# A two-layer trunk on one core: bias lines made by copies, small loads later, and three pieces of the schedule moved

## The chip, the cores and the metric

The kernel runs on one core of a Trainium2 chip. The metric is the device time of the whole execution in microseconds, as the median of several runs. One execution was also taken by the hardware profiler; its span runs from the first to the last instruction.

## The reference, cut to what matters

256 tokens of width 1024 pass two layers. Layer 0 is differential attention with eight pairs of heads, layer 1 is block attention, which at 256 tokens (one block) is plain causal attention with 16 heads on keys and values made from the stream. Each is followed by a squared-ReLU MLP of width 4096. Every softmax gets a bias from one table of 32 buckets by 16 heads, looked up by the distance of query and key; from a distance of 113 on, all fall into the last bucket.

```python
n = jnp.maximum(rel, 0)                       # rel = qpos - kpos
large = max_exact + (jnp.log(nf / max_exact) / math.log(128 / max_exact) * 16).astype(jnp.int32)
bucket = jnp.where(n < max_exact, n, jnp.minimum(large, 31))
...
# layer 0, per pair of heads m = 0, 1
s = einsum(q, k) + rel_bias[bucket]; s = where(rel >= 0, s, -inf); p = softmax(s)
a = p[:, :, 0] - lam * p[:, :, 1]
o = einsum(a, v)
o = o * rsqrt(mean(o * o) + eps) * subln_g * (1 - lam_init)
h = layer_norm(alpha * h + o @ w_out)
h = layer_norm(alpha * h + square(relu(h @ w_up)) @ w_down)
# layer 1: the same with plain softmax on shared keys and values
```

## The kernel before

All weights stream through on-chip memory as 96 units of 128 x 2048 fp32, each in two pieces of 128 x 1024. A product in fp32 is made of three matmuls in the fast fp32r format: a weight is split into `whi` (a rounded copy, by ACT, ScalarE) and `wlo` (what is left, by DVE, VectorE, as a subtraction), and an activation into `act_hi` and `act_lo` likewise. `three` (L134) issues the three matmuls, `fetch` (L82) loads a raw piece on SyncE's queue (SP) into one of five buffers, and `piece` (L103) splits one: it makes whi of this piece and the next on ACT, then wlo on DVE, then fetches the fifth piece on. `bg` calls it as often as the schedule says there, up to seven units ahead of use.

Nothing reorders the program: each engine runs its instructions as the code was written, so where a call stands in the code is where its parts stand on all engines. Transfers signal eight completion semaphores in turn (DMAHW0 to DMAHW7 in the listings), whether SP's or ACT's queue issued them.

The first two units are treated apart, by `v_first`: in eight chunks, k = 0 to 7, of 256 columns of x (transposed, `xT`) and 512 of the weight. For each, ACT makes act_hi and whi, DVE act_lo and wlo, and TensorE runs six matmuls of 512 columns. Ahead of that stands the head: DVE clears 512 columns (`zero`) and fills a table, TensorE runs four warm-up matmuls on the zeros (L177), the 33 x 384 one-hot matrix and the bias table are loaded on ACT's queue, and a matmul of the two (L183) gives for each of the 16 heads one line of 384 biases, by distance; the last 128 are the mask. DVE copies it out (L184), chunk 0 writes it to memory (`scr`, L363), and `load_bias` later reads from it, row by row one element further on, the 128 x 256 bias tile of a pair. The lambda vectors are loaded by GpSimd's queue at the start.

Attention in layer 0 goes by pairs of heads: `project` makes q and k, `halves_hi` and `halves_lo` split them, `scores` multiplies, `softmax_a` adds the bias and takes the maxima (DVE, L461 and L464) and the exponentials (ACT, L470), `softmax_b` puts the two maps together into `t` (DVE, L482), `turn` transposes t on TensorE (L503), `turned` copies that out as `aT`, and `values` multiplies with V (L527 to L529). Pairs 0 to 3 gather in O[0]: `rms` squares O (eight ACT operations, L563) and takes the reciprocal root on GpSimd (L253 and on), `scale` multiplies it in on DVE (L569), and `o_turn` transposes the scaled O on TensorE (L276) and splits it into act_hi (ACT) and act_lo (DVE, L73) for the output projection, `mix`.

In layer 1, `softmax_b` is a reciprocal and four scalings on DVE (L491, L494). In the MLP, `square` is a relu and a square on ACT (L737, L739), and `up_turn` transposes the result (L760).

Of the kernel before, what the change touches and what calls it, by code (L numbers as in the profile page):

```python
# [20 lines left out]
F32 = mybir.dt.float32  # L21
# [7 lines left out]
P = 128  # L29
D = 1024  # L30
# [3 lines left out]
NBUCKET = 32  # L34
# [18 lines left out]
def trunk(ctx: ExitStack, tc: tile.TileContext, x, xT, units, lam_a, subln, rel_bias,  # L53
          ln_g, ln_b, ident_in, onehot, out):
# [100 lines left out]
    early = wpool.tile([P, 2, D], F32, name="lnp").rearrange("p a b -> p (a b)")  # L155
    zero = early[:, 1024:1536]
    nc.vector.memset(zero, 0.0)
    oh = early[:, :RELS]
    table = const.tile([NBUCKET + 1, NH], F32, name="table")
    nc.vector.memset(table, 1.0)  # L160
    nc.scalar.dma_start(table[:NBUCKET], rel_bias)
    nc.scalar.dma_start(oh[:NBUCKET + 1], onehot)
    xres = const.tile([P, 2, D], F32, name="xres")
    xTr = xres.rearrange("p a b -> p (a b)")
    for k in range(NK):
        if k % 2 == 0:
            raws[k // 2] = wpool.tile([P, PIECE], F32, name="raw", bufs=RAWS)
        nc.sync.dma_start(xTr[:, k * S:(k + 1) * S], xT[:, k * S:(k + 1) * S])
        nc.sync.dma_start(raws[k // 2][:, (k % 2) * 512:(k % 2 + 1) * 512],
                          units[k // 4][:, (k % 4) * 512:(k % 4 + 1) * 512])  # L170
    fetch(4)
    ident = const.tile([P, P], F32, name="ident")
# [8 lines left out]
    pb = bank("c")  # L181
# [17 lines left out]

    def make_lambda():  # L200
        nc.gpsimd.dma_start(la, bass.AP(tensor=lam_a.tensor, offset=lam_a.offset,
                                        ap=[[0, P], [64, 4], [1, 64]]))
        nc.gpsimd.dma_start(gsub, subln.rearrange("o p -> p o"))
# [118 lines left out]
    def attention(layer, u0):  # L322
# [4 lines left out]
        with tc.tile_pool(name=f"attn{layer}", bufs=2) as pool, \  # L327
# [19 lines left out]
            def v_first(u):  # L347
# [7 lines left out]
                for k in range(4):  # L355
# [6 lines left out]
                    if kk == 0:  # L362
                        nc.scalar.dma_start(scr, line)  # L363
# [3 lines left out]
                    if kk < 2:  # L367
                        nc.tensor.matmul(warm[:, :P], zero[:, :P], zero[:, :P], start=True, stop=True)
# [8 lines left out]
            if layer == 0:  # L377
# [3 lines left out]
                nc.sync.dma_start(ident, ident_in)  # L381
                free.update(used)
# [242 lines left out]
            if diff:  # L625
# [48 lines left out]
            else:  # L674
# [16 lines left out]
                bg(2, True)  # L691
                softmax_b(7)
                values(6)
# [30 lines left out]
    def mlp(layer, u0, then):  # L724
# [3 lines left out]
        with tc.tile_pool(name=f"mlp{layer}", bufs=2) as pool:  # L728
# [87 lines left out]
            for g in range(2):  # L816
                up_rows(0, 1, g)
                bg(2)
# [151 lines left out]
```

## Time and profile before

| | us |
|---|---|
| median of 3 runs | 612.29 |
| lowest, highest | 611.0, 615.39 |
| the profiled execution | 612.53 |
| its span | 610.7 |
| TensorE busy in the span | 598.1 (98%), 3774 instructions |
| DVE, ACT, GpSimd busy | 379.4, 319.1, 9.8 |
| mean granted clock of TensorE | 0.995 of full |

TensorE is busy nearly all the time; the other engines have room on average, though not in each stretch. What lies outside the span is 1.8 us.

### The profile page before, as it was taken

How to read it: one execution, taken by the hardware profiler on the slowest of the kernel's cores; microseconds unless marked ns; L12 is line 12 of the kernel's file. 1: busy time of each engine (PE TensorE's matmuls, PEld its weight loads, DVE VectorE, ACT ScalarE, POOL GpSimd, SP SyncE). 2: the span in 40 equal slices, each digit the busy share in tenths (PEclk: the TensorE clock that was granted, in tenths of full speed). 3: DMA queues.
4: the chain of work that ended last, by engine and by line, in shares of the span. 5: the costliest groups of instructions: out<-in, count | busy, mean ns of one | idle time of the engine just before them, and what ended most of it. 6: DMA issues, size and time to landing. Idle time of an engine off the chain costs nothing.

```text
span 610.7 us, 9663 instructions
## 1 busy us (share of the span) xinstructions
PE 598.1 (98%) x3774; PEld 525.5 (86%) x3774; DVE 379.4 (62%) x694; ACT 319.1 (52%) x540; POOL 9.8 (2%) x29
## 2 busy tenths in 40 slices
PE   9999999999999999999999999999999999999994
PEld 6899987889898899898889999878798899899884
DVE  5597778976734734643777677687586544544236
ACT  5676687447654654552336555542686554564200
POOL 0000020000000000000000000000000000000000
PEclk9999999999999999999999999999999999999997
DMA  7996664547656657556149745151688556553001
GB/s 227 334 335 215 210 215 162 179 143 267 210 208 212 197 182 241 200 181 207 59 157 313 279 155 160 52 173 34 210 307 287 189 176 211 174 171 104 1 0 69
DMA packets 36408, 113.09 MB, mean 185 GB/s; under 512 B 3899, under 2 KB 9708, under 8 KB 36364
## 3 DMA queue, kind: packets, MB, share of 16 engines
q1 hardware_dynamic: 35008, 108.08, 53.0%
q0 software_dynamic: 1232, 4.33, 2.1%
q8 instruction: 29, 0.48, 0.3%
q10 hardware_dynamic: 124, 0.08, 0.1%
q14 instruction: 15, 0.12, 0.1%
HBM read 111.40 MB, written 1.07 MB: 184 GB/s over the span
## 4 chain that ended last, share of the span: by engine, by line
PE 79%; issue 9%; DMA 4%; DVE 3%; ACT 2%; POOL 1%; SPq 0%; DVEq 0%; POOLq 0%; ACTq 0%
PE ps_a L139 12%; PE ps_a L140 12%; PE ps_a L138 12%; PE ps_b L142 10%; PE ps_b L144 10%; PE ps_b L143 10%; PE ps_b L140 3%; PE ps_b L138 3%; PE ps_b L139 3%; DMA raw<-in_units 3%; DVE wlo L112 1%; PE ps_c L276 1%; PE ps_a L450 1%; PE ps_c L503 1%; DMA bias<-scr 1%
## 5 line engine op out<-in xcount | busy, mean ns | idle before, releaser
L112 DVE TENSOR_TENSOR wlo<-raw,whi 128x1024 fp32r<-128x1024 f32 x188 | 222.8, 1221 | 62.0 <-ACT whi L100 61.6
L100 ACT ACTIVATE whi<-raw 128x1024 fp32r<-128x1024 f32 x188 | 190.1, 1053 | 81.0 <-PE ps_a L140 50.5
L142 PE MATMUL ps_b<-act_hi,whi 128*128 128x256 f32 x640 | 182.4, 285 | 0.0
L144 PE MATMUL ps_b<-act_hi,wlo 128*128 128x256 f32 x640 | 180.2, 282 | 0.8 <-DVE wlo L112 0.8
L143 PE MATMUL ps_b<-act_lo,whi 128*128 128x256 f32 x640 | 179.9, 281 | 0.0
L142 PEld LDWEIGHTS ps_b<-act_hi,whi 128*128 128x128 f32 x640 | 120.5, 188 | 1.8 <-issue 0.7
L144 PEld LDWEIGHTS ps_b<-act_hi,wlo 128*128 128x128 f32 x640 | 120.5, 188 | 1.0 <-DVE wlo L112 1.0
L143 PEld LDWEIGHTS ps_b<-act_lo,whi 128*128 128x128 f32 x640 | 120.5, 188 | 0.5
L138 PE MATMUL ps_a<-whi,h_hi 128*128 128x512 f32 x248 | 98.5, 397 | 0.0
L140 PE MATMUL ps_a<-whi,h_lo 128*128 128x512 f32 x248 | 98.3, 396 | 0.0
L139 PE MATMUL ps_a<-wlo,h_hi 128*128 128x512 f32 x248 | 98.3, 396 | 0.0
L71 DVE TENSOR_TENSOR h_lo<-sqr,h_hi 128x512 fp32r<-128x512 f32 x24 | 16.6, 692 | 80.0 <-ACT h_hi L69 80.0
L140 PEld LDWEIGHTS ps_a<-whi,h_lo 128*128 128x128 f32 x248 | 46.7, 188 | 11.3
L139 PEld LDWEIGHTS ps_a<-wlo,h_hi 128*128 128x128 f32 x248 | 46.8, 189 | 10.8
L138 PEld LDWEIGHTS ps_a<-whi,h_hi 128*128 128x128 f32 x248 | 46.7, 188 | 10.8
L737 ACT ACTIVATE relu<-ps_b 128x512 f32<-128x512 f32 x32 | 19.1, 596 | 67.9 <-PE ps_b L144 57.7
L470 ACT ACTIVATE t<-t,mx 128x256 f32<-128x256 f32 x64 | 28.4, 445 | 30.9 <-DVE mx L467 30.9
L138 PE MATMUL ps_b<-whi,act_hi 128*128 128x512 f32 x96 | 39.2, 409 | 0.4 <-ACT act_hi L69 0.4
L140 PE MATMUL ps_b<-whi,act_lo 128*128 128x512 f32 x96 | 38.0, 396 | 0.5 <-DVE act_lo L73 0.5
L139 PE MATMUL ps_b<-wlo,act_hi 128*128 128x512 f32 x96 | 37.9, 395 | 0.0
L138 PE MATMUL ps_a<-whi,act_hi 128*128 128x512 f32 x80 | 32.4, 405 | 0.0
L140 PE MATMUL ps_a<-whi,act_lo 128*128 128x512 f32 x80 | 31.6, 395 | 0.0
(137 smaller groups left out, 591.7 us busy)
## 6 DMA issues: line engine op xcount, KB each, us to landing
raw<-in_units SPq DMA_DIRECT2D x188, 512.0 KB, 4.9
bias<-scr SPq DMA_DIRECT2D x16, 256.0 KB, 5.0
raw<-in_units SPq DMA_DIRECT2D x8, 256.0 KB, 5.5
lnp<-in_ln_g POOLq DMA_DIRECT2D x4, 512.0 KB, 3.9
lnp<-in_ln_b POOLq DMA_DIRECT2D x4, 512.0 KB, 5.1
xres<-in_xT SPq DMA_DIRECT2D x8, 128.0 KB, 4.4
xres<-in_x SPq DMA_DIRECT2D x1, 1024.0 KB, 6.8
out<-xres SPq DMA_DIRECT2D x2, 256.0 KB, 2.0
```

The source lines that it names most:

```text
L71: nc.vector.tensor_tensor(lo, src, hi.bitcast(F32), op=ALU.subtract)
L100: nc.scalar.activation(split[v][0][:, c], raws[state["head"]], AF.Copy)
L112: nc.vector.tensor_tensor(split[v][1][:, c], raws.pop(state["piece"]), split[v][0][:, c].bitcast(F32), op=ALU.subtract)
L138: nc.tensor.matmul(ps, a[0], w[0], start=start, stop=False)
L139: nc.tensor.matmul(ps, a[0], w[1], start=False, stop=False)
L140: nc.tensor.matmul(ps, a[1], w[0], start=False, stop=stop)
L142: nc.tensor.matmul(ps, w[0], a[0], start=start, stop=False)
L143: nc.tensor.matmul(ps, w[0], a[1], start=False, stop=False)
L144: nc.tensor.matmul(ps, w[1], a[0], start=False, stop=stop)
L276: nc.tensor.transpose(pt[:, j * P:(j + 1) * P], src[:, j * P:(j + 1) * P], ident)
L470: nc.scalar.activation(t[:, m, s], t[:, m, s], AF.Exp, bias=mx[:, m, j:j + 1], accum_out=sm[:, m, j:j + 1])
L737: nc.scalar.activation(r, ps, AF.Relu)
```

## The change

Four things change. **The head:** the first weight chunk is issued on ACT's queue; the one-hot matrix, its matmul, the copy and the table's filling go; the bias table, transposed to 16 x 32, is loaded behind that chunk on ACT's queue; and GpSimd builds the lines, with a memset for the mask, sixteen copies of one bucket's column over the run of distances that it covers, and one copy of sixteen buckets in reverse. Only 256 columns are cleared. The write of the lines moves from chunk 0 to chunk 6, the two warm matmuls inside chunks 0 and 1 go, and the lambda loads move to SP's queue, behind the identity matrix.

**The end of attention 0:** `rms` of O[0] moves ahead of a `bg(1)` and `softmax_b(6)`, `o_turn(0, ...)` moves ahead of the values of pairs 4 to 6, two pieces instead of three stand behind it, and the values of pairs 4 to 7 stand together ahead of `mix`. **Attention 1:** of two pieces ahead of `softmax_b(7)`, one moves behind it. **The MLP:** two pieces behind the last rows of the first chunk move behind `square` and `up_turn`.

```diff
-    oh = early[:, :RELS]
-    table = const.tile([NBUCKET + 1, NH], F32, name="table")
-    nc.vector.memset(table, 1.0)
-    nc.scalar.dma_start(table[:NBUCKET], rel_bias)
-    nc.scalar.dma_start(oh[:NBUCKET + 1], onehot)
...
-        nc.sync.dma_start(raws[k // 2][:, (k % 2) * 512:(k % 2 + 1) * 512],
-                          units[k // 4][:, (k % 4) * 512:(k % 4 + 1) * 512])
+        (nc.sync if k else nc.scalar).dma_start(raws[k // 2][:, (k % 2) * 512:(k % 2 + 1) * 512],
+                                                units[k // 4][:, (k % 4) * 512:(k % 4 + 1) * 512])
     fetch(4)
...
+    zero = early[:, 1024:1280]
+    nc.vector.memset(zero, 0.0)
+    table = early[:NH, :NBUCKET]
...
-    nc.tensor.matmul(pb[:NH, :RELS], table, oh[:NBUCKET + 1], start=True, stop=True)
-    nc.vector.tensor_copy(line, pb[:NH, :RELS])
+    def make_lines():
+        nc.scalar.dma_start(table, rel_bias)
+        nc.gpsimd.memset(line[:, 256:], MASKED)
+        b, half = _buckets(), NBUCKET // 2
+        runs = [j for j in range(256 - half) if j == 0 or b[j] != b[j - 1]] + [256 - half]
+        for c, d in zip(runs, runs[1:]):
+            nc.gpsimd.tensor_copy(line[:, c:d], table[:, b[c]:b[c] + 1].to_broadcast([NH, d - c]))
+        nc.gpsimd.tensor_copy(line[:, 256 - half:256], table[:, :half][:, ::-1])
...
+    def load_lambda():
+        nc.sync.dma_start(la, ...)
+        nc.sync.dma_start(gsub, subln.rearrange("o p -> p o"))
...
-                    if kk == 0:
+                    if kk == 6:
                         nc.scalar.dma_start(scr, line)
...
-                    if kk < 2:
-                        nc.tensor.matmul(warm[:, :P], zero[:, :P], zero[:, :P], start=True, stop=True)
...
                 nc.sync.dma_start(ident, ident_in)
+                load_lambda()
...
                 turned(5)
+                scale = rms(0, [O[0][:, h] for h in range(2)], nc.gpsimd)
                 bg(1)
                 softmax_b(6)
-                scale = rms(0, [O[0][:, h] for h in range(2)], nc.gpsimd)
                 bg(1)
...
                 turn(7)
-                for p in range(4, 7):
-                    values(p)
                 turned(7)
-                bg(3, True)
                 o_turn(0, 0)
                 o_turn(0, 1)
-                values(7)
+                bg(2, True)
+                for p in range(4, 8):
+                    values(p)
                 mix(0, 0, G0)
...
-                bg(2, True)
+                bg(1, True)
                 softmax_b(7)
+                bg(1, True)
...
-            for g in range(2):
-                up_rows(0, 1, g)
-                bg(2)
+            up_rows(0, 1, 0)
+            bg(2)
+            up_rows(0, 1, 1)
             SQ[0, 1] = square(SQ[0, 1])
             up_turn(1, 0)
+            bg(2)
```

ACT's first instructions before; `raw` is a weight chunk, `lnp` the buffer that holds one-hot matrix, lines and zeros, and what a row waits for stands in brackets:

```order
L162 DMA lnp<-in_onehot 33x384
L161 DMA table<-in_rel_bias 32x16 [waits DVE_49]
L69 ACT_TABLE_LOAD
L69 ACTIVATE act_hi<-xres 128x256 [waits DMAHW1_49]
L69 ACTIVATE whi<-raw 128x512 [waits DMAHW2_49]
L363 DMA scr<-lnp 16x384 [waits DVE_49]
L69 ACTIVATE act_hi<-xres 128x256 [waits DMAHW4_49]
L69 ACTIVATE whi<-raw 128x512 [waits DMAHW5_49]
```

The first five of them now, and, where the dots are, chunks 1 to 5 left out, the part around the write:

```order
L161 DMA raw<-in_units 128x512
L180 DMA lnp<-in_rel_bias 16x32
L69 ACT_TABLE_LOAD
L69 ACTIVATE act_hi<-xres 128x256 [waits DMAHW1_49]
L69 ACTIVATE whi<-raw 128x512 [waits DMAHW0_49]
...
L69 ACTIVATE whi<-raw 128x512 [waits DMAHW6_49]
L369 DMA scr<-lnp 16x384 [waits Pool_49]
L69 ACTIVATE act_hi<-xres 128x256 [waits DMAHW7_49]
L69 ACTIVATE whi<-raw 128x512 [waits DMAHW0_49]
L100 ACTIVATE whi<-raw 128x1024 [waits DMAHW1_49]
```

The write moved from behind chunk 0 to behind chunk 6 and waits for GpSimd instead of DVE; behind it stand chunk 7's two splits and the first whole piece.

ACT at the end of attention 0 before, from the copy of pair 5's aT to the exponentials of pair 7 (L470):

```order
L512 ACTIVATE aT<-ps_c 128x384 [waits PE_49]
L100 ACTIVATE whi<-raw 128x1024 [waits DMAHW2_49]
L563 ACTIVATE sq,ss<-o 128x128 [waits Activation_49]
L563 ACTIVATE sq,ss<-o 128x128
L563 ACTIVATE sq,ss<-o 128x128 [waits Activation_49] x6
L100 ACTIVATE whi<-raw 128x1024 [waits DMAHW5_49]
L512 ACTIVATE aT<-ps_c 128x384 [waits PE_49]
L470 ACTIVATE t,sm<-t,mx 128x256 [waits DVE_49]
```

The same stretch now:

```order
L517 ACTIVATE aT<-ps_c 128x384 [waits PE_49]
L568 ACTIVATE sq,ss<-o 128x128 [waits Activation_49]
L568 ACTIVATE sq,ss<-o 128x128
L568 ACTIVATE sq,ss<-o 128x128 [waits Activation_49] x6
L100 ACTIVATE whi<-raw 128x1024 [waits DMAHW3_49]
L100 ACTIVATE whi<-raw 128x1024 [waits DMAHW6_49]
L517 ACTIVATE aT<-ps_c 128x384 [waits PE_49]
L475 ACTIVATE t,sm<-t,mx 128x256 [waits DVE_49]
```

The eight squares moved ahead of the first of two whi. On DVE the wlo of that piece stands directly ahead of pair 7's maxima (L466 and L469), in both kernels; now:

```order
L112 TENSOR_TENSOR wlo<-raw,whi 128x1024 [waits DMAHW3_49,Activation_49]
L466 ISA t,mx<-ps_a,bias 128x256 [waits DMAHW5_49,PE_49]
L466 ISA mx 128x1
L469 ISA t,mx<-ps_a,bias 128x128
L469 ISA mx 128x1
```

Nothing moved in these five rows; the whi that the first of them waits for did.

TensorE a little later before, from the transposes of pair 7's t (L503) over the values of pairs 4 to 6 and O's eight transposes to the values of pair 7 and `mix`:

```order
L503 MATMUL ps_c<-ident,t 128x128 x3
L527 MATMUL ps_a<-V,aT 128x128
L528 MATMUL ps_a<-V,aT 128x128
L529 MATMUL ps_a<-V,aT 128x128
...
L276 MATMUL ps_c<-ident,o 128x128 x8
L527 MATMUL ps_a<-V,aT 128x128
L528 MATMUL ps_a<-V,aT 128x128
L529 MATMUL ps_a<-V,aT 128x128
L138 MATMUL ps_b<-whi,act_hi 128x512
```

Now:

```order
L508 MATMUL ps_c<-ident,t 128x128 x3
L282 MATMUL ps_c<-ident,o 128x128 x8
L532 MATMUL ps_a<-V,aT 128x128
L533 MATMUL ps_a<-V,aT 128x128
L534 MATMUL ps_a<-V,aT 128x128
...
L138 MATMUL ps_b<-whi,act_hi 128x512
```

O's transposes moved directly behind those of t, and all four groups of values stand between them and `mix`.

## Rows read from the trace of the kernel before

**Rows 1.** Waits of TensorE: operand, line, awaited engine: total us, times, longest.

```profile
PE ps_c L177 <- DVE table L160: 1.4, 1, 1.4
...
PE ps_c L760 <- ACT sqr L739: 0.3, 1, 0.3
```

**Rows 2.** Timeline of the head: start us, us, engine, line, operation, count, [idle before <-releaser].

```profile
1.16 0.43 SPq L169 DMA_DIRECT2D raw<-in_units  x1
...
1.44 3.78 PE L177 MATMUL ps_c<-lnp 128*128 128x256 f32 x8 [1.44 <-DVE table L160]
...
3.43 0.42 ACT L69 ACTIVATE act_hi<-xres 128x256 fp32r<-128x256 f32 x1 [0.34 <-DMA xres<-in_xT]
...
5.75 0.63 ACT L69 ACTIVATE whi<-raw 128x512 fp32r<-128x512 f32 x1 [1.91 <-DMA raw<-in_units]
...
6.54 1.22 PE L366 MATMUL ps_a<-whi,act_hi 128*128 128x512 f32 x2
...
8.85 1.05 PE L372 MATMUL ps_a<-wlo,act_hi 128*128 128x512 f32 x2
...
9.70 1.03 PE L366 MATMUL ps_a<-whi,act_hi 128*128 128x512 f32 x2
...
11.26 0.63 PE L372 MATMUL ps_a<-wlo,act_hi 128*128 128x512 f32 x2
...
11.72 0.63 PE L366 MATMUL ps_a<-whi,act_hi 128*128 128x512 f32 x2
...
19.06 1.06 ACT L100 ACTIVATE whi<-raw 128x1024 fp32r<-128x1024 f32 x1 [0.86 <-DMA raw<-in_units]
...
21.44 0.39 PE L144 MATMUL ps_b<-act_hi,wlo 128*128 128x256 f32 x1 [0.76 <-DVE wlo L112]
```

**Rows 3.** Transfers of the first 40 us: total; issue: count, KB each, us to landing.

```profile
DMA packets 5401, 11.36 MB, mean 284 GB/s; under 512 B 647, under 2 KB 2598, under 8 KB 5399
...
table<-in_rel_bias ACTq DMA_DIRECT2D x1, 2.0 KB, 3.2
```

**Rows 4.** Timeline of the end of attention 0, columns as in rows 2.

```profile
83.86 0.30 ACT L563 ACTIVATE sq<-o 128x128 f32<-128x128 f32 x1
...
85.33 0.42 DVE L461 CUSTOM_DVE_ANT_0 t<-ps_a,bias 128x256 f32<-128x256 f32 x1
...
86.20 1.05 ACT L100 ACTIVATE whi<-raw 128x1024 fp32r<-128x1024 f32 x1
...
87.52 0.51 ACT L470 ACTIVATE t<-t,mx 128x256 f32<-128x256 f32 x1
...
87.57 1.06 POOL L261 TENSOR_SCALAR rs_b<-rs_w 128x8 f32<-128x8 f32 x1
...
88.72 0.20 POOL L232 TENSOR_TENSOR rs_t<-rs_y 128x8 f32<-128x8 f32 x1
...
89.87 0.75 DVE L482 SCALAR_TENSOR_TENSOR t<-t,r 128x256 f32<-128x256 f32 x2
...
91.19 0.49 PE L503 MATMUL ps_c<-ident,t 128*128 128x128 f32 x3
...
91.61 1.29 DVE L569 TENSOR_TENSOR o<-o,rs_y 128x512 f32<-128x512 f32 x2 [0.90 <-POOL rs_y L241]
...
95.83 0.51 PE L138 MATMUL ps_b<-whi,act_hi 128*128 128x512 f32 x1 [0.43 <-ACT act_hi L69]
...
97.03 0.50 PE L140 MATMUL ps_b<-whi,act_lo 128*128 128x512 f32 x1 [0.45 <-DVE act_lo L73]
```

**Rows 5.** Timeline of attention 1 at the last transposes.

```profile
398.31 2.36 DVE L112 TENSOR_TENSOR wlo<-raw,whi 128x1024 fp32r<-128x1024 f32 x2 [0.25 <-ACT whi L100]
...
401.49 0.91 PE L503 MATMUL ps_c<-ident,t 128*128 128x128 f32 x6 [0.55 <-DVE t L494]
```

**Rows 6.** Timeline of the last MLP at the last transposes.

```profile
440.41 1.06 ACT L100 ACTIVATE whi<-raw 128x1024 fp32r<-128x1024 f32 x1 [1.45 <-DMA raw<-in_units]
...
442.67 0.65 PE L760 MATMUL ps_c<-ident,sqr 128*128 128x128 f32 x4 [0.28 <-ACT sqr L739]
```

More of the change, by code (lines that the diff above doesn't have):

```diff
@@ L53, in trunk @@
 def trunk(ctx: ExitStack, tc: tile.TileContext, x, xT, units, lam_a, subln, rel_bias,
-          ln_g, ln_b, ident_in, onehot, out):
+          ln_g, ln_b, ident_in, out):
     nc = tc.nc
@@ L153, in at @@
         return act[0][:, k, tokens(h)], act[1][:, k, tokens(h)]
-    early = wpool.tile([P, 2, D], F32, name="lnp").rearrange("p a b -> p (a b)")
-    zero = early[:, 1024:1536]
-    nc.vector.memset(zero, 0.0)
-    oh = early[:, :RELS]
-    table = const.tile([NBUCKET + 1, NH], F32, name="table")
-    nc.vector.memset(table, 1.0)
-    nc.scalar.dma_start(table[:NBUCKET], rel_bias)
-    nc.scalar.dma_start(oh[:NBUCKET + 1], onehot)
     xres = const.tile([P, 2, D], F32, name="xres")
@@ L168, in trunk @@
         nc.sync.dma_start(xTr[:, k * S:(k + 1) * S], xT[:, k * S:(k + 1) * S])
-        nc.sync.dma_start(raws[k // 2][:, (k % 2) * 512:(k % 2 + 1) * 512],
-                          units[k // 4][:, (k % 4) * 512:(k % 4 + 1) * 512])
+        (nc.sync if k else nc.scalar).dma_start(raws[k // 2][:, (k % 2) * 512:(k % 2 + 1) * 512],
+                                                units[k // 4][:, (k % 4) * 512:(k % 4 + 1) * 512])
     fetch(4)
+    early = wpool.tile([P, 2, D], F32, name="lnp").rearrange("p a b -> p (a b)")
+    zero = early[:, 1024:1280]
+    nc.vector.memset(zero, 0.0)
+    table = early[:NH, :NBUCKET]
     ident = const.tile([P, P], F32, name="ident")
@@ L180, in trunk @@
     line = early[:NH, 512:512 + RELS]
-    pb = bank("c")
-    nc.tensor.matmul(pb[:NH, :RELS], table, oh[:NBUCKET + 1], start=True, stop=True)
-    nc.vector.tensor_copy(line, pb[:NH, :RELS])
+    def make_lines():
[6 more added lines that the diff above has]
+        nc.gpsimd.tensor_copy(line[:, 256 - half:256], table[:, :half][:, ::-1])
+    make_lines()
     def load_bias(layer, p):
@@ L198, in trunk @@
     nlam = const.tile([P, 1], F32, name="nlam")
+    def load_lambda():
+        nc.sync.dma_start(la, bass.AP(tensor=lam_a.tensor, offset=lam_a.offset,
+                                      ap=[[0, P], [64, 4], [1, 64]]))
+        nc.sync.dma_start(gsub, subln.rearrange("o p -> p o"))
     def make_lambda():
-        nc.gpsimd.dma_start(la, bass.AP(tensor=lam_a.tensor, offset=lam_a.offset,
-                                        ap=[[0, P], [64, 4], [1, 64]]))
-        nc.gpsimd.dma_start(gsub, subln.rearrange("o p -> p o"))
         lp = small.tile([P, 2, 64], F32, name="lp", bufs=1)
@@ L917, in _layer_units, with _buckets @@
     return units
-def _onehot():
-    rel = 255 - np.arange(RELS)
-    n = np.maximum(rel, 0)
+def _buckets():
+    rel = 255 - np.arange(256)
     half = NBUCKET // 2
-    nf = np.maximum(n, half).astype(np.float32)
+    nf = np.maximum(rel, half).astype(np.float32)
     step = np.log(nf / np.float32(half)) / np.float32(math.log(MAXDIST / half)) * np.float32(NBUCKET - half)
     large = np.minimum(half + step.astype(np.int32), NBUCKET - 1)
-    bucket = np.where(n < half, n, large)
-    oh = np.zeros((NBUCKET + 1, RELS), np.float32)
-    ok = rel >= 0
-    oh[bucket[ok], np.arange(RELS)[ok]] = 1.0
-    oh[NBUCKET, ~ok] = MASKED
-    return oh
+    return [int(b) for b in np.where(rel < half, rel, large)]
 def kernel(x, w_in_a, lam_a, subln_a, w_out_a, w_kv_shared, w_q_b, w_out_b, rel_bias,
@@ L952 @@
         "subln": a["subln_a"],
-        "rel_bias": a["rel_bias"],
+        "rel_bias": a["rel_bias"].T,
         "ln_g": np.concatenate([a["ln1_g"], a["ln2_g"]]),
@@ L956 @@
         "ident": np.eye(P, dtype=np.float32),
-        "onehot": _onehot(),
     }
```

## Prediction

> **What bounds the kernel now.** I read the waits of the matmul engine first. There are six of them, from 1.4 us at the start to 0.3 us, 4.0 us in all [rows 1]: behind the head the engine is fed almost without a break, so an edit pays only where one of these waits or the start itself lies. No weight piece is late once the head is over; the change can win in the head and at three places behind it, and nowhere else.
>
> The head I read in order of time [rows 2]. Warm-up matmuls run from 1.44. The first piece of x arrives in time for ACT at 3.43, the first weight chunk only at 5.75 (ACT had waited 1.91 for it), and the first real matmul starts at 6.54, 0.8 later. Two pairs of matmuls start 0.85 apart at 8.85 and 9.70, so 0.43 us a matmul, which is the pace of the 1.2 GHz level; at 11.26 and 11.72 they are 0.46 apart, so 0.23 us, the pace of 2.4 GHz. The change of pace comes near 10.6, 4.0 us after the first real matmul and 9.1 after the first warm one. Then the first whole piece lands at 19.06, its difference comes late, and L144 waits 0.76 for it at 21.44. Two half-width matmuls of 0.12 us stand ahead of that one, so the unbroken stream begins in effect at 21.2. The head is what lies before this, and its gain is by how much 21.2 moves.
>
> **The head after.** The first chunk is issued on ACT's queue beside x, not 0.43 us behind it on SP's. Its landing is not in the trace of before. Early bound: as soon as x's 128 KB, 3.4. Late bound: only one issue is saved, 5.75 - 0.43 = 5.3. Both fight for the same transfers and the chunk is twice as large, but the 49.5 KB one-hot and the 128 KB lambda transfer no longer start beside it; I take the middle, 4.35, and the first real matmul at 5.15. The bias matmul between warm-up and real work and the two warm ones inside chunks 0 and 1 are gone, and ACT no longer stands at the bias write after chunk 0.
>
> Eight chunks are 48 matmuls. For the change of pace I have two bounds: 4.0 us after the first real matmul, 9.15, or 9.1 us after the first warm one (now near 1.2), 10.3. By the first, 9.3 matmuls run at 0.43 and 38.7 at 0.233: 5.15 + 4.0 + 9.0 = 18.2. By the second, 12 and 36: 18.7. I take 18.2, as the real matmuls begin earlier and with nothing mixed in. Could the data hold this up? The first whole piece is number nine: eight times 384 KB and 512 KB, 3.67 MB, at the mean 284 GB/s of the first 40 us [rows 3] 12.9 us, and 2.4 us later (19.06 to 21.44) its difference is there: 15.3, well before 18.2. Even a landing at 15.5 would be hidden. So 21.2 becomes 18.2: **minus 3.0**, bounds 2.0 (below, the late landing) and 4.9 (no slow matmul: 5.15 + 11.2 = 16.3).
>
> What the moved steps add: seventeen GpSimd copies after the table lands. The table took 3.2 us from its issue [rows 3]; issued at 1.3 to 1.4 it is there at 4.6. GpSimd's small operations last 0.20 in the clear [rows 4], 0.3 with what lies between; then the lines are done at 9.7, ahead of chunk 6, and the write costs its issue only. The lambda loads now stand on SP's queue behind the bias load, which waits for the write; piece fetches queue behind them, but the five buffers ahead are already under way by then and lambda is wanted much later. I cost that at nothing; cover gone, it is a late piece of some 2 us in the second or third unit.
>
> **End of attention 0.** Before, O's turn ends in two waits: 0.43 for act_hi at 95.83, then L140 at 97.03, 1.20 behind L138 where two steps of 0.233 are due, so 0.73 [rows 4]: 1.16 in all. Now O is turned before the values of pairs 4 to 7, which cover both splits; the 1.16 goes. But what is late next? The order shows the eight squares moved ahead of the first small piece on ACT. They take 2.34 us (83.86 to 86.20). That piece's whi then ends near 86.25 instead of 83.9, and its difference (1.23) stands on DVE directly ahead of pair 7's maxima, which started at 85.33: they start at 87.5. They need about 1.4, so the exponentials begin at 88.9 instead of 87.52, and t, written from 89.87 for 0.75, is complete at 92.0 instead of 90.6. The engine wants it at 91.19: it had 0.6 to spare and now loses 0.85. Next on the matmul engine is no longer 2 us of values but O's transposes, and DVE scales O's halves only behind t (1.29 for two): ready at 92.85 and 93.5. The three transposes of t are done at 92.4, so 0.45 and then 0.15 more are lost. Together 1.45 lost for 1.16 won: **plus 0.3**. Bounds: minus 1.16 if the difference does not hold the maxima, plus 0.8 if GpSimd's rsqrt, which starts 1 us earlier but meets one more DVE subtraction, ends after t.
>
> **Attention 1 and the MLP.** L503 waits 0.55 for t because two differences (2.36) stand ahead of it on DVE [rows 5]. One of them, 1.2, goes behind; t is then there before the matmuls end. **Minus 0.6**; the second difference delays a copy of aT that has a stretch of projection to hide in. In the last MLP the square that L760 waits 0.28 for started late because two whi ahead of it on ACT waited for their pieces, the last at 440.41 for 1.45 [rows 6]. The square now stands ahead of both. The wait and the drain before it go: **minus 0.35**. Bounds 0.3 to 0.7 and 0.25 to 0.45.
>
> **Sum.** The profiled execution took 612.53, 0.2 above the median 612.29: 612.53 - 3.0 + 0.3 - 0.6 - 0.35 = **608.9**, 0.55% faster. One per cent, 6.1 us, is about what a measurement of this kernel can tell from no change.
>
> **Rivals.** (1) O's turn pays in full: the difference finds its whi early, or pair 7 has more slack than I count. For it: the loss hangs on a chain of five steps, and 0.6 us less in it halves it. Against it: the order, in which the maxima cannot pass the difference. -1.16 in place of +0.3: 607.4.
>
> (2) The pace rises earlier, since nothing now breaks the real matmuls. Half of the slow stretch: 2.0 us at 0.43 are 4.65 matmuls, 43.35 more take 10.1, end 17.25: 607.95. For it: the bias matmul and the mixed-in warm ones are gone. Against it: in before the engine was busy from 1.44 without bringing the change any sooner.
>
> (3) The second queue saves only an issue. First matmul at 6.1, pace up at 10.1, end 19.15, head gain 2.0: 609.9. For it: in before the chunk needed 4.6 us from its issue, of which the issue took 0.43, so most of its time is the transfer. The Trainium skill, "DMA: Bandwidth & Descriptors", section "Issuing engines are not separate DMA queues", says that transfers issued on several engines share the same 16 DMA engines and that only the issue time is saved. By that rule the sum is 609.9; no row of before tells, as no weight transfer left on ACT's queue there.
>
> (4) **Slower**: the bias lines come too late. The write stands on ACT's queue ahead of chunk 7's two splits and the first whole piece's whi. If the lines are done at T, issue, splits, whi and difference take 3.65, and the stream begins at about T + 3.4. With c us a copy T = 4.6 + 17c. Up to c = 0.60 nothing is lost; the head's gain is gone at T = 17.8, c = 0.78; with the 0.65 won behind it, the kernel is slower from T = 18.45, c = 0.81. One row speaks for such a price: GpSimd's L261 lasted 1.06 beside a DVE subtraction, while its fellow at 88.72 took 0.20 [rows 4], and DVE's head is full of subtractions. At 1.06 each: T = 22.6, stream at 26.0, 612.53 + 4.8 - 0.65 = 616.7. Against it: the head's subtractions work on 256 and 512 columns, not 1024, so one wait would be about half as long (0.5 to 0.6, still hidden), and not every copy need meet one. The Trainium skill, "SBUF — State Buffer", section "Who interferes with whom", states that a DVE instruction with two SBUF inputs locks out a GpSimd instruction that reads SBUF; that row agrees, and the rule bears against this change.
>
> **How the numbers follow.** Forecast 0.48, (1) 0.12, (2) 0.15, (3) 0.15, (4) 0.10. The range 606.3 to 611.4 holds cases (1) to (3), the forecast's bounds and the mild end of (4) (c = 0.75 gives 611.4); both (1) and (2), or a head near its 4.9, lie at or below its lower end. Over 1% faster needs 606.2: 0.12. Over 1% slower needs T = 24.3, c = 1.16: 0.03. Within 1%: 0.85.
>
> **What would show it.** In the profile after: first real matmul near 5.1; full pace near 9.2; a stream without breaks from about 18; GpSimd's copies over before 10 and no wait on ACT ahead of the write; a new wait of the matmul engine for t, then for O's scaling, near what was 91; no wait at the layer-1 transposes of t, none for the square. Wrong would make it: copies of over 0.60 us, a pace that rises at another time than I took, or pair 7's maxima that start on time.

## The result, and the profile after

The changed kernel takes 605.61 us (median of 4 runs, 602.79 to 607.19); the kernel before, measured beside it, 613.13. The ratio is 0.9875, interval 0.9846 to 0.9904: 1.25% faster, where 0.55% was forecast, and 0.7 us below the lower end of the range. The profiled execution took 604.83 with a span of 602.8, so 2.0 us lie outside (1.8 before). The granted clock is 0.995 in both.

Waits of the matmul engine after (operand, line, awaited engine: total us, times, longest), to be read against [rows 1]:

```profile
PE ps_c L173 <- DVE lnp L166: 1.2, 1, 1.2
PE ps_c L508 <- ACT V L339: 1.0, 1, 1.0
PE ps_b L142 <- ACT relu L742: 0.9, 1, 0.9
PE ps_b L144 <- DVE wlo L112: 0.8, 1, 0.8
PE ps_a L372 <- ACT whi L69: 0.5, 1, 0.5
PE ps_b L142 <- ACT whi L100: 0.2, 1, 0.2
PE ps_a L455 <- ACT qh L435: 0.2, 1, 0.2
PE ps_c L282 <- DVE o L574: 0.2, 1, 0.2
```

They sum to 5.0 us, against 4.0 before. The kernel became 7.9 us shorter in span and waits longer: the reader should stop here, because no list of waits can hold this gain. Four waits of before are gone (t in attention 1, both splits of O, the square), six have come. What shrank is the work itself. Groups by line and shape, before (columns: out<-in, shapes, count | busy us, mean ns of one | idle):

```profile
L143 PE MATMUL ps_b<-act_lo,whi 128*128 128x256 f32 x640 | 179.9, 281 | 0.0
...
L139 PE MATMUL ps_a<-wlo,h_hi 128*128 128x512 f32 x248 | 98.3, 396 | 0.0
```

The same view after:

```profile
L143 PE MATMUL ps_b<-act_lo,whi 128*128 128x256 f32 x640 | 178.7, 279 | 0.0
...
L139 PE MATMUL ps_a<-wlo,h_hi 128*128 128x512 f32 x248 | 98.3, 396 | 0.0
```

The 640 matmuls of 256 columns take 279 ns each instead of 281, those of 512 columns on `h` as long as before. Matmuls overlap, so their rate is read from one start to the next. Before, in the first full unit:

```profile
21.66 0.28 PE L142 MATMUL ps_b<-act_hi,whi 128*128 128x256 f32 x1
...
23.09 0.28 PE L142 MATMUL ps_b<-act_hi,whi 128*128 128x256 f32 x1
```

After, the same twelve steps:

```profile
20.00 0.28 PE L142 MATMUL ps_b<-act_hi,whi 128*128 128x256 f32 x1
...
21.36 0.28 PE L142 MATMUL ps_b<-act_hi,whi 128*128 128x256 f32 x1
```

Twelve steps take 1.43 us before and 1.36 after: 119 ns and 113 ns a matmul, with nothing waiting and the same clock. Averaged over a whole trace (all distances from one start to the next that are no wait), the step of the 1920 matmuls of 256 columns fell from 118.6 to 116.3 ns, 4.4 us in all, and that of some 1240 matmuls of 512 columns from 233.6 to 232.2, 1.7 us. Nothing in my prediction contains these 6.1 us.

**The head after** (timeline, columns as in [rows 2]):

```profile
0.74 0.41 ACTq L161 DMA_DIRECT2D raw<-in_units  x1
...
4.12 0.63 ACT L69 ACTIVATE whi<-raw 128x512 fp32r<-128x512 f32 x1
4.53 3.45 POOL L185 COPY lnp<-lnp 16x143 f32<-16x143 f32 x16 [3.60 <-DMA lnp<-in_rel_bias]
4.80 1.18 PE L372 MATMUL ps_a<-whi,act_hi 128*128 128x512 f32 x2
5.82 0.63 PE L374 MATMUL ps_a<-whi,act_lo 128*128 128x512 f32 x2
6.28 0.63 PE L376 MATMUL ps_a<-wlo,act_hi 128*128 128x512 f32 x2
7.37 0.42 ACT L69 ACTIVATE act_hi<-xres 128x256 fp32r<-128x256 f32 x1 [1.56 <-DMA xres<-in_xT]
...
15.28 0.63 ACT L69 ACTIVATE whi<-raw 128x512 fp32r<-128x512 f32 x1 [2.04 <-DMA raw<-in_units]
16.71 1.06 ACT L100 ACTIVATE whi<-raw 128x1024 fp32r<-128x1024 f32 x1 [0.80 <-DMA raw<-in_units]
...
19.08 0.38 PE L144 MATMUL ps_b<-act_hi,wlo 128*128 128x256 f32 x1 [0.76 <-DVE wlo L112]
19.48 0.42 SPq L205 DMA_DIRECT2D lnp<-in_lam_a  x1
...
27.28 1.06 ACT L100 ACTIVATE whi<-raw 128x1024 fp32r<-128x1024 f32 x1 [3.36 <-DMA raw<-in_units]
```

The first chunk is split at 4.12 without a wait, the first real matmul starts at 4.80, and the pairs at 5.82 and 6.28 are already 0.23 us a matmul. From 7.37 on the rows name transfers: chunk 2 waits for x, chunk 7 waits 2.04 for its weight, the first whole piece lands at 16.71, and L144 starts 2.4 us behind it. The stream is steady from 18.85 (by the reckoning that gave 21.2 before), and ACT then stands 3.36 us for a piece, ahead of which the lambda loads had been issued.

**The end of attention 0 after** (timeline, against [rows 4]):

```profile
82.47 1.99 ACT L100 ACTIVATE whi<-raw 128x1024 fp32r<-128x1024 f32 x2
...
83.54 1.23 DVE L112 TENSOR_TENSOR wlo<-raw,whi 128x1024 fp32r<-128x1024 f32 x1 [2.38 <-ACT whi L100]
83.55 1.31 POOL L266 TENSOR_SCALAR rs_a<-rs_w 128x8 f32<-128x8 f32 x1
...
84.68 0.42 DVE L466 CUSTOM_DVE_ANT_0 t<-ps_a,bias 128x256 f32<-128x256 f32 x1
...
88.49 0.77 DVE L487 SCALAR_TENSOR_TENSOR t<-t,r 128x256 f32<-128x256 f32 x2
...
89.25 1.28 DVE L574 TENSOR_TENSOR o<-o,rs_y 128x512 f32<-128x512 f32 x2
89.41 0.52 PE L508 MATMUL ps_c<-ident,t 128*128 128x128 f32 x3 [1.01 <-ACT V L339]
...
90.08 1.23 PE L282 MATMUL ps_c<-ident,o 128*128 128x128 f32 x8 [0.15 <-DVE o L574]
```

The chain is the one worked out ahead: the piece's difference waits 2.38 for a whi that stands behind the squares, the maxima wait for the difference, and t is complete at 89.26. The wait at 89.41 is put down to the copy of V, but that ran on ACT from 88.83 for other data, and t's last part ended at 89.26: it was t.

**Attention 1 and the last MLP after** (timeline, against [rows 5] and [rows 6]):

```profile
394.56 1.22 DVE L112 TENSOR_TENSOR wlo<-raw,whi 128x1024 fp32r<-128x1024 f32 x1
394.69 0.49 PE L508 MATMUL ps_c<-ident,t 128*128 128x128 f32 x3
...
440.35 1.06 ACT L100 ACTIVATE whi<-raw 128x1024 fp32r<-128x1024 f32 x1 [1.07 <-DMA raw<-in_units]
...
441.32 0.58 ACT L742 ACTIVATE relu<-ps_b 128x512 f32<-128x512 f32 x1
441.95 0.39 PE L142 MATMUL ps_b<-act_hi,whi 128*128 128x256 f32 x1 [0.87 <-ACT relu L742]
```

L508 follows without a wait; the second difference now starts behind t. In the MLP the square of the first rows is early, but the relu of the next ones stands behind a whi that waits 1.07 for its piece, and the engine waits for that instead.

### The profile page after: what moved, and what is told of

Read it like the earlier page. It is cut to its first block, busy times and chain, and to the rows that moved or that the text cites. A ratio compares the mean times of both kernels' runs of the same rounds, so it can differ in the third digit from the quotient of the medians.

```text
span 602.8 us, 9665 instructions
## 1 busy us (share of the span) xinstructions
PE 589.3 (98%) x3768; PEld 519.3 (86%) x3768; DVE 378.5 (63%) x692; ACT 319.2 (53%) x540; POOL 13.9 (2%) x45
## 3 DMA queue, kind: packets, MB, share of 16 engines
HBM read 111.35 MB, written 1.07 MB: 186 GB/s over the span
## 4 chain that ended last, share of the span: by engine, by line
PE 88%; DMA 5%; ACT 3%; DVE 2%; issue 1%; SPq 1%; DVEq 0%; ACTq 0%
PE ps_a L138 12%; PE ps_a L140 12%; PE ps_a L139 12%; PE ps_b L142 12%; PE ps_b L144 11%; PE ps_b L143 11%; DMA raw<-in_units 4%; PE ps_b L138 4%; PE ps_b L140 4%; PE ps_b L139 4%; PE ps_a L455 2%; PE ps_c L282 1%; PE ps_c L508 1%; DMA scr<-lnp 1%; ACT whi L100 1%; PE ps_a L543 1%
## 5 line engine op out<-in xcount | busy, mean ns | idle before, releaser
L144 PE MATMUL ps_b<-act_hi,wlo 128*128 128x256 f32 x640 | 178.8, 279 | 0.8 <-DVE wlo L112 0.8
L144 PEld LDWEIGHTS ps_b<-act_hi,wlo 128*128 128x128 f32 x640 | 121.5, 190 | 1.0 <-DVE wlo L112 1.0
L140 PE MATMUL ps_a<-whi,h_lo 128*128 128x512 f32 x248 | 98.2, 396 | 0.0
L140 PEld LDWEIGHTS ps_a<-whi,h_lo 128*128 128x128 f32 x248 | 46.7, 188 | 11.3
L742 ACT ACTIVATE relu<-ps_b 128x512 f32<-128x512 f32 x32 | 19.1, 596 | 66.7 <-PE ps_b L144 56.3
L140 PE MATMUL ps_b<-whi,act_lo 128*128 128x512 f32 x96 | 37.7, 393 | 0.0
L140 PE MATMUL ps_a<-whi,act_lo 128*128 128x512 f32 x80 | 31.4, 393 | 0.0
```

Source lines behind the costliest of these rows:

```text
L140: nc.tensor.matmul(ps, a[1], w[0], start=False, stop=stop)
L144: nc.tensor.matmul(ps, w[1], a[0], start=False, stop=stop)
L742: nc.scalar.activation(r, ps, AF.Relu)
```

## Experiments

What removing a tile does to addresses: the 64 bytes of `table` lay ahead of nearly all buffers, so without it everything behind the activations (`act_hi`, `act_lo`) moved down by 64 bytes. In the laid-out program act_hi begins at byte 16512 of each partition in both kernels and the first weight buffer whi at 70400 before and 70336 after; all weight buffers are a multiple of 256 apart, and so are act_hi and act_lo, and h_hi and h_lo. I call (weights − activations) mod 256 the distance: 53888 leaves 128 before, 53824 leaves 64 after. For the MLP's `h` it is 160 in both, since both moved. Ratios are to the kernel before, which was run beside each group of experiments (612.58, 612.10, 612.79, 612.25, 612.21).

**e1**, the changed kernel once more: 

> The changed kernel once more, nothing edited. The waits of its trace account for only about 1 us of the 7.5; the rest lies in shorter steps between matmuls (256 columns: 113 to 118 ns after, 118.6 before). Placement theory (the 64-byte table is gone, so every weight buffer lies 64 bytes lower): the same short steps again, 605 +- 2. Execution theory (the step differs from execution to execution): another mix of steps, and times that reach up to 609 or 610. Schedule theory (the order of the instructions sets the step): as placement, 605 +- 2.

Measured 605.85, ratio 0.9886 (0.9857 to 0.9916). The result stands. A second trace shows the spread between executions: the first transposes of t start at 44.27 here, at 40.94 in the other trace.

**e2**, the 64 bytes put back, unused:

```diff
+    pad = const.tile([NBUCKET + 1, NH], F32, name="pad")
+    nc.gpsimd.memset(pad, 0.0)
```

> The changed kernel with an unused 64-byte tile where the table stood, so that all buffers behind it lie where they lay before. Placement theory: steps of 118.6 ns again, and 611 to 612. Execution and schedule theory: no change, 605 +- 2.

Measured 610.15, 0.9955 (0.9936 to 0.9974), and the steps are those of before again. So 4.3 us of the gain (against e1) hang on 64 bytes that nobody reads, and the schedule alone is worth 2.4 us by the medians (1.6 to 3.9 by the ratio), where 3.65 was forecast.

**e3**, the kernel before with its table inside another tile, the schedule untouched:

```diff
-    table = const.tile([NBUCKET + 1, NH], F32, name="table")
+    table = early[:NBUCKET + 1, 896:896 + NH]
```

> The kernel before with its table moved into a free part of the buffer that holds the one-hot matrix, so that all later buffers lie 64 bytes lower, as in the changed kernel; the schedule is that of before. Placement theory: steps of 113 to 118 ns, 606 to 607. Execution and schedule theory: no change, 612 to 613.

Measured 607.85, 0.9921 (0.9892 to 0.9950): 4.7 us from a change of address. Two waits of its trace are longer than before:

```profile
PE ps_c L760 <- ACT sqr L739: 1.8, 1, 1.8
...
PE ps_b L140 <- DVE act_lo L73: 1.1, 1, 1.1
```

They were 0.3 in [rows 1] and 0.45 in [rows 4]. A faster stream does not explain them. At L140, e11 and e15 wait 0.8 with steps of 118.6 and 119.3; at L760, e14 waits 0.4 with steps shorter than here. The traced execution took 611.8, 4 us above the median, so a wait that is seen here alone proves little.

**e4**, the changed head alone, the three later pieces as before (the diff's parts on `rms`, `o_turn`, `bg` and `up_rows` undone): 

> The changed kernel's head alone; the three later pieces of the schedule as before. From the waits of the trace after: the three pieces together cost it about 0.5 us (attention 0 plus 0.4, attention 1 minus 0.7, MLP plus 0.6), so 605 +- 1.5 by every theory of the step; if the three pieces carry the gain, 611.

Measured 608.75, 0.9926 (0.9912 to 0.9941). Neither expected value came: the later pieces are worth 2.9 us at this placement, against e1.

**e11**, e4 with e2's pad: 

> The changed head alone, with the 64 bytes put back, so with buffers placed as before. The prediction's head term is minus 3.0, which would give 609.4. By the transfers (a dip from 20 to 24 us, and the pieces that the first scores wait for no earlier than before) it is less: minus 0.5 to minus 1.5, 611 to 612.

Measured 612.18, 0.9984 (0.9968 to 1.0000). At the old addresses the new head brings 0.6 us by the medians and 0 to 2.0 by the ratio, an interval that just reaches no change; I had forecast 3.0.

**e5, e6, e12**, other distances, the schedule that of the changed kernel. e5 puts e2's pad ahead of the activations, so that they and the weights both move by 64; e6 widens the pad to 128 bytes (shown) and e12 narrows it to 32 (`[NBUCKET + 1, 8]`):

```diff
-    pad = const.tile([NBUCKET + 1, NH], F32, name="pad")
+    pad = const.tile([NBUCKET + 1, 2 * NH], F32, name="pad")
```

> The changed kernel with a 64-byte tile ahead of the activations: activations and weights both lie 64 bytes higher, so their distance is that of the changed kernel, while the weights lie where they lay before. If the weights' own place sets the step: 118.7 ns for 256 columns and 610. If the distance between activations and weights does: 113 to 118 ns and 606.

> The changed kernel with 128 bytes where the table stood: the weights lie 128 bytes higher than in it, 64 higher than before. If the step repeats every 128 bytes: 113 to 118 ns and 606, as the changed kernel. If it is a matter of lying lower or of the total: 118.7 ns and 610 or more.

> The changed kernel with 32 bytes where the table stood: weights and activations 96 bytes apart (counted in 256), where the changed kernel has 64 and before had 128. If any distance off a multiple of 128 will do: 113 to 118 ns for 256 columns and 605. If 64 is special: near 118.7 ns and 608 to 610.

Measured 604.71, 0.9887 (0.9865 to 0.9909); 604.87, 0.9884 (0.9859 to 0.9910); 609.18, 0.9939 (0.9918 to 0.9961). e5 has the weights where they lay before and is fast: their own address alone doesn't set the step, and the distance fits. That it should be counted in 256 bytes is my choice; 64 and 192 differ, so it does not repeat every 128, and no run tests 256. At 192 the 256-column step is shorter still, the 512-column one is not, and in sum it equals 64; 96 is nearly as slow as 128.

**e10**, 96 bytes ahead of the MLP's own buffers, which moves `h`, and with it the buffers of relu and its square, and leaves weights and act_hi alone (distance of h: 160 to 64):

```diff
+            gap = pool.tile([P, 24], F32, name="gap", bufs=1)
+            nc.gpsimd.memset(gap, 0.0)
```

> The changed kernel with a gap of 96 bytes ahead of the MLP's hidden activations, so that they stand to the weights (64 bytes apart, counted in 256) as the attention's activations do in the changed kernel; the down products had 234.3 ns for 512 columns in both kernels, and their distance was the same in both. Distance theory: the down products step like the changed kernel's other 512-column products, 229 to 230 ns, 744 of them, so 3 to 4 us won: 601 to 602.5. If it is only a matter of the attention's buffers: 234.3 ns and 605.

Measured 598.73, 0.9770 (0.9743 to 0.9797): 7 us below the changed kernel, from a tile that nobody reads. Groups by line and shape, as above:

```profile
L143 PE MATMUL ps_b<-act_lo,whi 128*128 128x256 f32 x640 | 177.8, 278 | 0.0
...
L139 PE MATMUL ps_a<-wlo,h_hi 128*128 128x512 f32 x248 | 97.2, 392 | 0.0
```

Here both groups are shorter. In the timeline, six steps of the down product after, and then in e10:

```profile
200.09 0.39 PE L138 MATMUL ps_a<-whi,h_hi 128*128 128x512 f32 x1
...
201.49 0.40 PE L138 MATMUL ps_a<-whi,h_hi 128*128 128x512 f32 x1
```

```profile
200.27 0.39 PE L138 MATMUL ps_a<-whi,h_hi 128*128 128x512 f32 x1
...
201.65 0.39 PE L138 MATMUL ps_a<-whi,h_hi 128*128 128x512 f32 x1
```

1.40 against 1.38 us. Over the whole trace the 512-column step fell from 232.2 to 229.1 ns, 3.8 us; and the 256-column step from 116.3 to 114.9, 2.8 us, although nothing that those matmuls read had moved.

**e17**, the control: the same tile and memset, but behind the other buffers, so that nothing moves: 

> A control for e10: the changed kernel with the same 96-byte tile and the same GpSimd memset, but the tile lies behind the MLP's other buffers, so nothing that an engine reads is moved. Theory of placement: the time of the changed kernel, 605.6, and 234 ns for the 512-column step. Rival, that the extra tile or its memset (another instruction, another wait) makes the gain: 598.7.

Measured 607.44, 0.9930 (0.9905 to 0.9956), the steps of the changed kernel. No gain (1.8 above the changed kernel's median): it is the place.

**e16, e18**, other distances of h, by gaps of 160 and 32 bytes (`[P, 40]`, `[P, 8]`): 

> The changed kernel with a gap of 160 bytes: weights and hidden activations at the same place modulo 256 (distance 0). Seen so far: 64 and 192 fast, 96, 128 and 160 slow. If what decides is the distance from 64 or 192, distance 0 is slow, 234 ns, and the time that of the changed kernel, 605.6. If 128 is special (slow near 128, fast elsewhere), distance 0 is fast, 226-231 ns, and 598.7.

> The changed kernel with a gap of 32 bytes ahead of the MLP's activations: the hidden activations then begin at a multiple of 64 bytes (in the changed kernel 32 past one), and their distance from the weights is 128 modulo 256. The slow distances so far are 128 (both at multiples of 64), 96 and 160 (one of the two 32 past a multiple). If being a multiple of 64 is all that counts for the hidden activations: fast, near 599 to 602. If distance 128 is slow in itself, as between weights and attention's activations: 234 ns and 605.6.

Measured 602.48, 0.9841 (0.9814 to 0.9867), and 605.24, 0.9885 (0.9866 to 0.9903). Distance 0 has the shortest 512-column step of all, 227.9, so the expectation that only 64 and 192 are fast fell; 128, both operands at multiples of 64, lies between it and 160. In e16 the 256-column step stayed at 116.1, and only about half of e10's 7 us are there.

**e14, e15**, the kernel before, its whole schedule kept, with e3's and e10's edits together, and with e10's alone: 

> The kernel before, whole schedule unchanged, with both placements: the bias table inside another tile (weights 64 bytes lower, as in e3) and the 96-byte gap ahead of the MLP's activations (as in e10). Theory of placement: both gains add, 612.8 - 4.7 - 7.1 = 601.0, and what is then left to e10 (598.7) is the schedule, 2 to 3 us. Rival, the gains need the new schedule (its stream without breaks): then 604 or more.

> The kernel before with the 96-byte gap alone: weights against attention's activations stay at 128 bytes, against the MLP's hidden ones go from 160 to 64. Theory: only the down products get faster, 512-column step 234 to 226-231 ns, the 256-column step of the up products stays at 118.6; 612.8 - 7 = 605.8. Rival, that one distance decides for all products: no gain, 612.8.

Measured 598.98, 0.9785 (0.9766 to 0.9805), and 610.47, 0.9973 (0.9964 to 0.9983). e14 is the plainest answer to what the addresses are worth, though half of it, the move of h, is no part of the change's own gain: without one moved instruction the old kernel comes to 599.0, as fast as the changed one with the same gap (598.73). The steps account for it: 1926 times 4.2 ns and some 1240 times 4.4 ns are 13.5 us; the medians differ by 13.3, the two traced executions by 14.4. e15 refutes that each product has its own distance and nothing else: the 512-column step fell as expected, but the 256-column one rose, and 1.8 us are left of the 7. The rise is in the MLP alone (118.6 to 119.8 ns; attention stays at 118.6).

The steps and times side by side (steps: mean distance from start to start over one trace; A: distance to attention's activations, H: to h):

| kernel | A, H | 256 columns, ns | 512 columns, ns | time, us |
|---|---|---|---|---|
| before | 128, 160 | 118.6 | 233.6 | 612.3 |
| e2, new schedule | 128, 160 | 118.6 | 233.6 | 610.2 |
| e12, new schedule | 96, 160 | 117.9 | 233.8 | 609.2 |
| e3, old schedule | 64, 160 | 116.7 | 232.3 | 607.9 |
| after | 64, 160 | 116.3 | 232.2 | 605.6 |
| e5, new schedule | 64, 160 | 116.5 | 232.2 | 604.7 |
| e6, new schedule | 192, 160 | 115.1 | 233.8 | 604.9 |
| e18, new schedule | 64, 128 | 116.7 | 231.2 | 605.2 |
| e16, new schedule | 64, 0 | 116.1 | 227.9 | 602.5 |
| e10, new schedule | 64, 64 | 114.9 | 229.1 | 598.7 |
| e14, old schedule | 64, 64 | 114.4 | 229.2 | 599.0 |
| e15, old schedule | 128, 64 | 119.3 | 230.7 | 610.5 |

The 512-column means mix two kinds of product, and apart they are simpler. Over all traces, products that read act_hi and act_lo step at 229.2 to 229.6 ns with A 64, 232.6 to 232.8 with 128 and 233.2 to 233.3 with 96 and 192. The down products step at 226.8 with H 0, 228.9 to 229.2 with 64, 232.2 with 128 and 234.1 to 234.2 with 160. Where runs share one distance and differ in the other, they stay within these bounds. So for 512 columns each product does follow its own distance; the 256-column steps do not.

**e7**, the lambda loads on GpSimd's queue, as before the change (`nc.gpsimd.dma_start` for both): 

> The changed kernel with the two lambda loads on GpSimd's queue again, not on SP's behind the bias load. Queue theory (the loads of bias, identity and lambda on SP push the weight pieces behind them back: 162 GB/s from 20 to 24 us where before had 307): the dip is half filled, the wait of 1.0 at the first scores shrinks below 0.5, and 0.5 to 1.5 us are won. Rival (the lambda load only moves into the first 10 us, where it delays the chunks, as the 120 GB/s from 4 to 6 us of before suggest): the first chunks come 0.5 to 1 us later and the time stays within 0.5.

Measured 604.63, 0.9883 (0.9861 to 0.9905). By windows (us, busy time of PE, PEld, DVE, ACT, GpSimd, clock, DMA share, GB/s), after and then e7:

```profile
20.00:24.00 4.00, 4.00 (x38) 4.00 (x37) 3.85 (x4) 3.49 (x5) 0.00 (x0) 1.00 0.60 162
```

```profile
20.00:24.00 4.00, 4.00 (x37) 4.00 (x37) 3.86 (x4) 3.49 (x5) 0.00 (x0) 1.00 0.97 319
```

The small loads on SP's queue, ahead of the pieces, halve what moves in these 4 us (162 against 319; e1, with the loads on SP's queue, has 205). Without them the first scores don't wait; the gain of 1.0 (against 605.61) is within the spread.

**e9**, the write of the bias lines behind chunk 3 instead of 6 (`if kk == 3`): 

> The changed kernel with the lines written behind chunk 3, not chunk 6. The copies were done at 8.3 and the write, issued at 12.3, landed at about 18.5, which is what the bias load and all fetches behind it on SP waited for. Queue theory: written near 10, it lands by 16, the bias load goes out at 17.0 directly behind the piece fetches, and the fetches behind come 1.5 us earlier: 0.5 to 1.5 us won. Rival (the write waits for the copies and stops ACT, or the data rate sets the pace anyway): within 0.5 of the changed kernel.

Measured 604.48, 0.9884 (0.9855 to 0.9913), no different: the bias load is still issued at 18.33, behind the pieces ahead of it on SP's queue. The late write costs nothing.

**e8**, `rms` behind the `bg(1)` again, so that the small piece's whi comes ahead of the squares, O's turn as changed:

```diff
+                bg(1)
                 scale = rms(0, [O[0][:, h] for h in range(2)], nc.gpsimd)
-                bg(1)
                 softmax_b(6)
```

> The changed kernel with the small piece ahead of the eight squares on ACT again. By the prediction's chain pair 7's maxima then start on time and t is there before its transposes: the gap of 1.2 to 1.4 us ahead of them goes, and the wait for O's scaling behind them grows to 0.5 to 1.2, as GpSimd's rsqrt starts 1 us later: 0.3 to 1 us won in that stretch, 604.5 to 605.5 in all. If t was not what they waited for (the trace names the copy of V), the gap stays.

Measured 604.98, 0.9878 (0.9846 to 0.9911). The wait at the transposes of t is gone (they start at 88.14), and O's turn waits instead:

```profile
90.00 1.23 PE L282 MATMUL ps_c<-ident,o 128*128 128x128 f32 x8 [1.37 <-DVE o L574]
```

Both orders reach the values at the same point (91.06 here, 91.14 after): with O turned first, O's scaling is the next thing late, whichever piece goes ahead.

**e13**, e10 with e7's edit: 

> The changed kernel with the 96-byte gap of e10 ahead of the MLP's activations, and with the lambda loads on GpSimd's queue, as in e7. If placement and the queue are separate causes, the two add: e10's 598.7 less the 0.3 to 1.2 us that e7 stood below the changed kernel, so 597.5 to 598.4, the first scores without their wait, and the 512-column step of the down products at 226 to 231 ns. If e7's difference was only the spread between executions, 598.7. Rival: the head's time is set by the transfers as a whole, so that what lambda no longer delays is delayed by something else; then it stays at 598.7 with another wait.

Measured 597.46, 0.9763 (0.9744 to 0.9782), the fastest version. Its interval and e14's overlap: at this placement the whole schedule change and the lambda move are worth about 1.5 us of 599, which these runs hardly tell from nothing.

## Why the prediction was wrong

**The step that failed is the first one**, "the change can win in the head and at three places behind it, and nowhere else". It took the pace of an engine that is always busy as given. The part on the change then lists the table's filling as removed, but not the table: its 64 bytes moved the weights against the activations. Worth 4.3 us by e2, 4.7 by e3, more than all the moved work. Among my rivals was no such case. The steps stood in the trace of before, 0.119 and 0.233, and I used them as constants.

**Head, forecast −3.0.** First matmul 4.80 (5.15 forecast), full pace from 5.8 (9.15 forecast), so rival 2 was right about the pace and wrong about what follows: the pace no longer bounds. The failed term is the answer to "Could the data hold this up?". It put the ninth landing at 12.9 by the mean rate, from zero, as if transfers ran from the first instant and in the order of need; it came at 16.71, and 16.71 + 2.4 is the 19.1 of L144. By its windows this trace moved 300 GB/s from 2.00 to 16.71, so 4.4 MB and not the 3.67 MB counted. Over all traces L144 starts at 19.85 to 22.34 with the old head (four traces, mean 21.4) and at 17.62 to 21.07 with the new (sixteen, mean 19.1): 2.3 earlier, within my bounds. But I followed the gain no further. The lambda loads were costed at nothing; the pieces behind them come late, and by the first transposes of t the means are 42.9 and 41.6: 1.3 is left, with ranges that overlap (40.92 to 43.79 and 40.09 to 44.27), and e11's time shows about that or less.

The old head can also run quickly. In e14 its first pair of real matmuls lasts 0.73, where [rows 2] has 1.22, and then it waits for data as the new one does:

```profile
5.80 0.73 PE L366 MATMUL ps_a<-whi,act_hi 128*128 128x512 f32 x2
...
8.70 0.72 PE L366 MATMUL ps_a<-whi,act_hi 128*128 128x512 f32 x2 [0.86 <-ACT whi L69]
...
19.85 0.38 PE L144 MATMUL ps_b<-act_hi,wlo 128*128 128x256 f32 x1 [0.76 <-DVE wlo L112]
```

My 10.6 for the pace was one execution's, not the head's property. Rival 3, a second queue that saves only an issue, was wrong for the first chunk, which was ready at 4.12 or earlier (no run parts the queue from the transfers that no longer start beside it). Its end of the head, 19.15, is near the measured 18.85 by luck: its pace rose at 10.1 and the data was no bound, where the pace rose at 5.8 and the data was late. The Trainium skill, "DMA: Bandwidth & Descriptors", section "Issuing engines are not separate DMA queues", states that DMAs of all queues run on the same 16 DMA engines and interleave there. The trace agrees: their share is 0.95 from 2.00 to 16.71, so what all queues move together sets the landing at 16.71.

**GpSimd's copies.** Sixteen took 3.45 us, 0.22 each on average; rival 4, which needed 0.81, is refuted. The long operation it argued from is real: at 83.55 a small GpSimd operation lasted 1.31 beside a DVE subtraction, as in [rows 4], and the head's copies show it too. Three of the sixteen ran nearly all their time beside a subtraction and lasted 0.75, 0.39 and 0.65; of the rest, the first took 0.29 and the others 0.18 each. One of either kind, with the subtraction:

```profile
4.77 0.75 POOL L185 COPY lnp<-lnp 16x14 f32<-16x14 f32 x1
4.78 0.69 DVE L71 TENSOR_TENSOR wlo<-raw,whi 128x512 fp32r<-128x512 f32 x1 [0.27 <-ACT whi L69]
...
7.17 0.18 POOL L185 COPY lnp<-lnp 16x4 f32<-16x4 f32 x1
```

So the prediction's own argument against rival 4 holds: the subtractions are shorter, and most copies meet none.

**End of attention 0, forecast +0.3.** The mechanism held row by row: t late (1.40 from the last product's start where 0.23 is due, so 1.17; forecast 0.85), O's scaling late (0.32 and 0.14 above the 0.11 of such a step; forecast 0.45 and 0.15). Yet from the transposes of pair 6 to the first turn behind `mix` it took 18.43 before and 18.37 after, 18.37 in e2 too: more was lost than I counted and more was won. The other traces show a win. With the old order e4, e11, e14 and e15 take 18.77 to 18.87, and L140 waits 0.80 to 1.06 there; with the new order all fourteen, e8 among them, take 18.37 to 18.51. So about 0.4 is won where I forecast 0.3 lost. The mis-sized term is the 1.16 that goes: it was read from one execution, in which L140 waited only 0.45.

**Attention 1, forecast −0.6.** From the last turn of t but one to the last it takes 8.00 before (393.49 to the 401.49 of [rows 5]), 7.25 to 7.42 with the new order (after, e1, e2, e12) and 8.0 without (e3, e4, e11): right. **Last MLP, forecast −0.35.** The wait is gone and another of up to 0.9 came, for the next relu behind the next late piece: nothing on balance at the old addresses (18.35 before and 18.62 in e11, 18.66 in e2); after and e1 have 18.65 and 18.28, e4 with the old order 18.80. I named no "what is late next" for this one, and "No weight piece is late once the head is over" was wrong already in [rows 6], where ACT waits 1.45 for one.

So at the old addresses, each against the kernel before beside it: −0.6 for the head (e11; −1.3 by the landmark) and −2.4 in all (e2), which leaves −1.8 for the rest. Forecast were −3.0, −3.65 and −0.65: the sum is nearer than its terms, because a head far too large stands beside a rest too small. The addresses bring 4.3 to 4.7 on top. By the stretches of e11 and e2 the later pieces bring 0.41 in attention 0 and 0.71 in attention 1, 1.1 of the 1.8; the remainder stays open.

**What stays open** is the rule behind the steps. The table says which placements are fast here, not why: the same shape has several steps within one trace (some 113 and 118 ns for 256 columns in the changed kernel), and the up products answered to a move of h, which they don't read. The gaps moved the buffers of relu and its square by as much as h, and no run moves either alone.

## What to carry to other kernels

Where the main engine is busy 98% of the time, look at the distance from one instruction's start to the next before looking at waits: here a few nanoseconds on thousands of matmuls outweighed every stall in the list. Any edit that adds, drops or resizes a tile moves all that lies behind it, so time it against a variant with the old addresses (an unused tile of the same size), and then try a few gaps on purpose. A gain in the head counts only at the first landmark that the next transfers don't take back, and one profiled execution doesn't tell it when executions differ there by 3 us.

## What the runs showed of the hardware

The rate of fp32r matmuls depended on where their operands lay in a partition: between the kernel before and e14, with the same program order, the mean step fell from 118.6 to 114.4 ns and from 233.6 to 229.2, and the time by 2.15% (1.95 to 2.34). The granted clock of the profiled execution lay between 0.992 and 0.997 in every kernel and doesn't show it. For 512 columns it went with the distance of weights and activations, in the down products from 226.8 ns at 0 to 234.2 at 160.

The time at which the matmul engine passes to the pace of the 2.4 GHz level came near 5.8 us in e14 and near 10.6 before, with the same instructions ahead of it, and the granted clock of the profile's windows reads 1.00 throughout.

A GpSimd copy of 16 rows that ran beside a DVE subtraction of 512 columns lasted 0.65 and 0.75 us, and 0.18 where none ran.
